# First layer: x and its norm placed ahead of the state tables, scale and shift by halves of the channels, the first products of w_in in two halves

## The chip, the cores and the metric

The kernel runs on one core of a Trainium2 chip. The time is the device time of one execution in microseconds (us), and of several executions the median is given. The core has TensorE (PE; its weight loads are listed as PEld), VectorE (DVE), ScalarE (ACT), GpSimd (POOL) and SyncE (SP), which here only issues DMA transfers. ACT issues DMA transfers too, on a queue of its own.

## The reference

A network of two layers on 256 tokens of 1024 channels, all in fp32. Each layer normalizes x, scales and shifts it by values that come from a conditioning vector c, runs a mixer (an S5 state-space layer in layer 0, an attention layer in layer 1), and then a PEER mixture of experts in the same manner:

```python
def rmsnorm(x, g):
    y = x * lax.rsqrt(jnp.mean(x * x, axis=-1, keepdims=True) + RMS_EPS)
    return y * g
...
    c_act = jax.nn.silu(c)
    for i in range(DEPTH):
        mod = c_act @ ada_w[i] + ada_b[i]
        sh1, sc1, g1, sh2, sc2, g2 = jnp.split(mod, 6, axis=-1)
        hm = rmsnorm(x, norm1_g[i]) * (1.0 + sc1) + sh1
        y = s5_mixer(hm, ...) if i % 2 == 0 else nsa_mixer(hm, ...)
        x = x + g1 * y
        hf = rmsnorm(x, norm2_g[i]) * (1.0 + sc2) + sh2
        x = x + g2 * peer(hf, ...)
    return rmsnorm(x, final_g)
...
def s5_mixer(h, w_in, a_re, a_im, log_dt, b_re, b_im, c_re, c_im, d_skip, w_glu):
    u = h @ w_in
    # powers of exp(a * dt), times b and c, give a recurrence over the tokens for each of 64 groups
```

## The kernel before

x is held transposed in one tile `xT`: 128 partitions by 8 chunks (k) of 128 channels by 256 tokens. Products with the big weights are made of three fp32r products (`mm3`, L188 to L190): a weight block of 128x1024 arrives in a buffer `raw` (`load_unit`, L129, a 512 KB transfer on SP's queue into one of six buffers), ACT rounds it to `w_hi` in two halves of four chunks (L139), DVE subtracts to get `w_lo` (L181), and PE adds w_hi x h_hi, w_hi x h_lo and w_lo x h_hi.

What the start of layer 0 has to make, and the lines that the profile shows for it:

- `Tables(K, pp)` clears the tiles of the state tables. `s5_params` (L359 to L420) turns the parameters in `prm` into coefficients: on ACT an exp (L383), a tanh (L387) and two sines (L395, L396), on DVE a long run of 128x32 operations.
- `sq_all`: eight squares of xT on ACT (L249) and their sums over the channels on PE (L260, products with ones).
- `ada_block(K, 0, n)`: 512 of the 6144 values of mod. Four loads of ada_w, eight products with the column `cact` = silu(c) (L201), a row copied by ACT (L204); the call of what it returns (`ada_turn`) turns the row by products with ones (L213), and DVE adds the bias into `mod` (L216). Blocks 0 and 1 are the shift for chunks 0 to 3 and 4 to 7, blocks 2 and 3 the scale. silu is made of a sigmoid on ACT (L118) and a DVE product (L119).
- `rms_scale`: mean on DVE (L273), square root on ACT (L274), reciprocal and a diagonal on DVE (L275, L277), and a PE product with ones (L279) that spreads the result over the partitions: `rs`, in PSUM.
- `Norm`: `nsc` = (1 + scale) * g on DVE (L290); `scaled(k)` makes `nt` = xT * nsc * rs on DVE (L297); `shifted(k)` adds the shift, `h_hi` on ACT (L303) and `h_lo` on DVE (L304).
- `tab.first(0)`: angles, sines and cosines of the first quarter of the groups (L464 to L475), `bpad` by complex products on DVE and POOL (L450 to L455), its 16 PE transposes (L489) and four ACT copies to `win` (L490). `tab.second(0)`: `wo` (L501, L455) and T (L512 on PE, L516 on ACT).
- `Pair`: loads and splits of the first two blocks of w_in; `add(k)` makes the six products of chunk k.

`tc.manual_schedule(engines={PE, Activation})` in `s5_layer` keeps the instructions of the block on PE and ACT in the order in which they are written. DVE, POOL, SP and everything outside the block is ordered by the compiler's planner, which goes by simulated time and priority; `high_priority(offset=...)` raises what stands in it. Within a queue, every engine works in order. `s5_mix` then goes through the eight blocks of w_in with the states of each, and the tables of later quarters; the planner places some of their DVE and ACT work before that.

Of the kernel before, what the change touches and what calls it, by code (L numbers as in the profile page):

```python
# [14 lines left out]
OP = mybir.AluOpType  # L15
# [5 lines left out]
KC = D // P  # L21
DEPTH = 2
EPS = 1e-6
PRIO = 200
# [85 lines left out]
def small(K, name):  # L110
    o, w = SMALLS[name]
    return K.sm[:, o:o + w]
# [9 lines left out]
def bank(K):  # L122
    return K.ps.tile([P, 512], F32, name="bank")


def load_unit(K, src):

    t = K.st.tile([P, 1024], F32, name="raw", bufs=RAW)
    K.nc.sync.dma_start(t, src)  # L129
    return t  # L130
# [13 lines left out]
def split_w(K, raw):  # L144

    with K.tc.high_priority(offset=PRIO):
        return [split(K, raw[:, i * 512:(i + 1) * 512], [P, 512], "w", bufs=4) for i in range(2)]
# [10 lines left out]
class Pair:  # L158


    def __init__(self, K, srcs, x):
        self.K, self.x = K, x
        self.ws = [split_w(K, load_unit(K, src)) for src in srcs]
        self.ps = [bank(K)[:, :S] for _ in srcs]
# [28 lines left out]
def ada_block(K, layer, n):  # L193

    nc = K.nc
    ps = bank(K)
    for k2 in range(KC // 2):
        w = load_unit(K, K.aps["ada_w"][n, k2]).rearrange("p (k n) -> p k n", k=2)
        for i in range(2):
            k = 2 * k2 + i  # L200
            nc.tensor.matmul(ps[32 * (k % 4):32 * (k % 4) + 32], K.cact[:, k, :], w[:, i, :],  # L201
                             start=(k < 4), stop=(k >= 4), skip_group_check=True)
    row = K.xp.tile([P, 512], F32, name="ada_row", bufs=1)
    nc.scalar.activation(row, ps, AF.Copy)  # L204
    return lambda: ada_turn(K, layer, n, row)
# [58 lines left out]
def sq_all(K):  # L264
    for k in range(KC):
        sq_add(K, k)


def rms_scale(K):

    nc = K.nc
    ms = K.xp.tile([P, 2], F32, name="ms")
    nc.vector.tensor_scalar(ms, K.sq[:, 0:2], 1.0 / D, EPS, op0=OP.mult, op1=OP.add)  # L273
    nc.scalar.activation(ms, ms, AF.Sqrt)  # L274
    nc.vector.reciprocal(ms, ms)  # L275
    diag = K.xp.tile([P, 2, P], F32, name="rs")
    nc.vector.tensor_mul(diag, K.ident[:, None].to_broadcast([P, 2, P]), ms[:, :, None].to_broadcast([P, 2, P]))  # L277
    rs = bank(K)[:, :S]
    nc.tensor.matmul(rs, K.ones, diag.rearrange("p t n -> p (t n)"), start=True, stop=True)  # L279
    return rs  # L280


class Norm:


    def __init__(self, K, g, layer, part, rs, bufs=4):
        self.K, self.part, self.rs, self.bufs = K, part, rs, bufs
        self.mod = K.mod[layer]
        self.sc = K.xp.tile([P, KC], F32, name="nsc")
        K.nc.vector.scalar_tensor_tensor(self.sc, self.mod[:, part + 8:part + 16], 1.0, g, op0=OP.add, op1=OP.mult)  # L290
        self.hi = K.hpool.tile([P, KC, S], F32R, name="h_hi")
        self.lo = K.hpool.tile([P, KC, S], F32R, name="h_lo")
        self.t = K.xp.tile([P, KC, S], F32, name="nt")

    def scaled(self, k):
        K = self.K
        K.nc.vector.scalar_tensor_tensor(self.t[:, k % self.bufs], K.xT[:, k], self.sc[:, k:k + 1], self.rs,  # L297
                                         op0=OP.mult, op1=OP.mult)
# [29 lines left out]
NP2 = 32  # L328
# [7 lines left out]
S5_W = 3 * NP2 + 4 * NP2 * 16  # L336
# [185 lines left out]
def s5_layer(K):  # L522
    tc, nc = K.tc, K.nc
    with tc.tile_pool(name="s5p", bufs=1, reuse_waits="tile") as pp:
        prm = pp.tile([P, S5_W], F32, name="prm")
        nc.sync.dma_start(prm, K.aps["s5p"])
        nc.sync.dma_start(K.xT, K.aps["xT"])
        tab = Tables(K, pp)
        with tc.manual_schedule(engines={mybir.EngineType.PE, mybir.EngineType.Activation}):
            s5_params(K, pp, prm)  # L530
            sq_all(K)
            ada_block(K, 0, 2)()
            ada_block(K, 0, 3)()
            rs = rms_scale(K)
            tab.first(0)
            norm = Norm(K, small(K, "n1g")[:, 0:8], 0, 0, rs, KC)
            with tc.high_priority(offset=2 * PRIO):
                for k in range(KC):
                    norm.scaled(k)
            h = (norm.hi, norm.lo)  # L540
            ada_block(K, 0, 0)()
            pair = Pair(K, [K.aps["w_in"][0], K.aps["w_in"][1]], h)
            ada_block(K, 0, 1)()
            with tc.high_priority(offset=2 * PRIO):
                for k in range(4):
                    norm.shifted(k)
            with tc.high_priority(offset=2 * PRIO):
                for k in range(4, KC):
                    norm.shifted(k)
            for k in range(4):  # L550
                pair.add(k)
            for k in range(4, KC):
                pair.add(k)
            tab.second(0)
        s5_mix(K, pp, h, tab, pair.ps)

# [860 lines left out]
```

## Time and profile before

| | us |
|---|---|
| median of 3 runs | 2096.19 |
| lowest, highest | 2095.28, 2097.87 |
| the profiled execution, its own time | 2095.41 |
| its span from the first to the last instruction | 2093.6 |
| PE busy | 2036.0 (97%) |
| DVE busy | 1611.3 (77%) |
| ACT busy | 1154.3 (55%) |

The profile is one execution, recorded by the hardware. Times in it count from the start of the span. A busy share is an average over the whole span; the first 57 us, which the change touches, look different from the rest. "Idle before" is the time in which the engine had nothing running ahead of a row's first instruction, with the engine and line that ended it. Landings of a transfer are given from its issue. DMA from a queue runs on 16 DMA engines.

### The profile page before, as it was taken

What the parts mean: (1) busy time and instruction counts of PE and PEld (TensorE: products, weight loads), DVE (VectorE), ACT (ScalarE), POOL (GpSimd) and SP (SyncE); (2) the same over time, 40 slices, a digit from 0 to 9 for tenths busy, and PEclk for the clock granted to TensorE, in tenths of its full rate; (3) what the DMA queues carried; (4) which work ended last, traced back from release to release, by engine and by line L of the source; (5) the groups of instructions that cost most, each with busy time, mean ns of one, the idle gap of its engine ahead of it and who ended that gap; (6) DMA issues with size and microseconds to landing.
All of it is one profiled execution on the core that took longest, in us unless ns stands there. A gap on an engine that the chain in (4) does not pass through costs nothing. (4 is left out here: it accounts for less than half of the span.)

```text
span 2093.6 us, 39285 instructions
## 1 busy us (share of the span) xinstructions
PE 2036.0 (97%) x14344; PEld 1842.8 (88%) x14344; DVE 1611.3 (77%) x3698; ACT 1154.3 (55%) x2396; POOL 113.3 (5%) x149
## 2 busy tenths in 40 slices
PE   6899999999999999999999999999999999999998
PEld 3789999899999988888888689999999998888887
DVE  8696899878887777777766769998788865566555
ACT  4775555554445555555545655555454455555554
POOL 4220001200000000000010000022000000000000
PEclk9899999999999999999999999999999999999999
DMA  7445555544446788888863035555444455666663
GB/s 282 149 180 162 162 173 172 160 151 135 140 140 190 260 271 274 267 269 272 270 221 101 21 129 165 172 171 162 141 132 142 141 177 184 194 193 196 193 192 100
DMA packets 102690, 377.18 MB, mean 180 GB/s; under 512 B 11488, under 2 KB 11872, under 8 KB 101472
## 3 DMA queue, kind: packets, MB, share of 16 engines
q1 hardware_dynamic: 101520, 371.42, 55.8%
q0 software_dynamic: 544, 2.61, 0.4%
q8 instruction: 112, 1.84, 0.3%
q14 instruction: 82, 0.67, 0.1%
q10 hardware_dynamic: 432, 0.65, 0.1%
HBM read 373.07 MB, written 1.05 MB: 179 GB/s over the span
## 5 line engine op out<-in xcount | busy, mean ns | idle before, releaser
L139 ACT ACTIVATE w_hi<-raw 128x512 fp32r<-128x512 f32 x1194 | 746.8, 628 | 737.8 <-PE bank L189 433.5
L181 DVE TENSOR_TENSOR w_lo<-raw,w_hi 128x512 fp32r<-128x512 f32 x1194 | 814.9, 704 | 132.5 <-ACT w_hi L139 130.2
L188 PE MATMUL bank<-h_hi,w_hi 128*128 128x256 f32 x2504 | 717.3, 289 | 9.0 <-ACT w_hi L139 5.6
L190 PE MATMUL bank<-h_hi,w_lo 128*128 128x256 f32 x2504 | 709.1, 286 | 10.7 <-DVE w_lo L181 10.7
L189 PE MATMUL bank<-h_lo,w_hi 128*128 128x256 f32 x2504 | 709.5, 284 | 1.4 <-DVE h_lo L304 1.4
L188 PEld LDWEIGHTS bank<-h_hi,w_hi 128*128 128x128 f32 x2504 | 485.2, 195 | 17.1 <-ACT w_hi L139 7.5
L190 PEld LDWEIGHTS bank<-h_hi,w_lo 128*128 128x128 f32 x2504 | 480.2, 193 | 15.3 <-DVE w_lo L181 14.7
L189 PEld LDWEIGHTS bank<-h_lo,w_hi 128*128 128x128 f32 x2504 | 483.1, 193 | 3.8 <-DVE h_lo L304 2.7
L799 PE MATMUL bank<-w_lo,a_hi 128*128 128x512 f32 x1024 | 399.0, 390 | 0.2 <-DVE w_lo L181 0.2
L799 PE MATMUL bank<-w_hi,a_lo 128*128 128x512 f32 x1024 | 398.5, 389 | 0.0
L799 PE MATMUL bank<-w_hi,a_hi 128*128 128x512 f32 x1024 | 281.0, 390 | 0.0
L181 DVE TENSOR_TENSOR a_lo<-B,a_hi 128x256 fp32r<-128x256 f32 x256 | 108.9, 425 | 197.9 <-ACT a_hi L139 197.8
L799 PEld LDWEIGHTS bank<-w_hi,a_lo 128*128 128x128 f32 x1024 | 192.3, 188 | 39.8
L799 PEld LDWEIGHTS bank<-w_lo,a_hi 128*128 128x128 f32 x1024 | 192.3, 188 | 39.8 <-DVE w_lo L181 0.7
L799 PEld LDWEIGHTS bank<-w_hi,a_hi 128*128 128x128 f32 x1024 | 191.5, 188 | 38.6
L770 PE MATMUL bank<-ohl,oij 128*128 128x128 f16 x1024 | 129.2, 307 | 0.0
L139 ACT ACTIVATE a_hi<-B 128x256 fp32r<-128x256 f32 x256 | 106.7, 418 | 27.0 <-PE bank L799 14.4
L773 DVE SCALAR_TENSOR_TENSOR B<-bank,B 128x216 f32<-128x216 f32 (+31 forms) x128 | 62.5, 488 | 71.9 <-PE bank L770 71.1
L770 PEld LDWEIGHTS <-oij 128*128 128x128 f16 x1024 | 101.5, 128 | 4.2
L762 DVE TENSOR_TENSOR oij<-iota,slotT 128x1024 f16<-128x1024 f16 x128 | 89.2, 698 | 0.0
L765 DVE TENSOR_TENSOR ohl<-oij,slotT 128x1024 f16<-128x1024 f16 x128 | 88.8, 695 | 0.1
L233 DVE SCALAR_TENSOR_TENSOR raw<-raw,cb 128x1024 f32<-128x1024 f32 x56 | 68.3, 1219 | 0.0
(263 smaller groups left out, 1790.2 us busy)
## 6 DMA issues: line engine op xcount, KB each, us to landing
raw<-peer_u SPq DMA_DIRECT2D x256, 512.0 KB, 3.6
raw<-peer_v SPq DMA_DIRECT2D x256, 512.0 KB, 4.3
raw<-ada_t SPq DMA_DIRECT2D x56, 512.0 KB, 4.6
raw<-ada_w SPq DMA_DIRECT2D x40, 512.0 KB, 5.4
raw<-w_q SPq DMA_DIRECT2D x32, 512.0 KB, 3.5
raw<-w_glu SPq DMA_DIRECT2D x16, 512.0 KB, 4.1
raw<-w_in SPq DMA_DIRECT2D x8, 512.0 KB, 6.3
w<-w_cmp SPq DMA_DIRECT2D x4, 1024.0 KB, 9.4
```

Source lines behind the costliest of these rows:

```text
L139: nc.scalar.activation(hi, raw, AF.Copy)
L181: K.nc.vector.tensor_tensor(lo, raw, hi.bitcast(F32), op=OP.subtract)
L188: nc.tensor.matmul(out, wh, xh, start=start, stop=False)
L189: nc.tensor.matmul(out, wh, xl, start=False, stop=False)
L190: nc.tensor.matmul(out, wl, xh, start=False, stop=stop)
L233: V.scalar_tensor_tensor(w, w, 1.0, cb, op0=OP.mult, op1=OP.mult, accum_out=part[:, m:m + 1])
L762: V.tensor_tensor(oij.rearrange("p a n j t -> p (a n) j t"), tab[:, None].to_broadcast(full), si, op=OP.is_equal)
L765: V.tensor_tensor(ohl, oj, slotT[:, 1, 2 * q:2 * q + 2, :, None, :].to_broadcast([P, 2, 2, P, 2]), op=OP.mult)
L770: nc.tensor.matmul(pv[:, :, t], oij[:, t // 2, 0, :, t % 2], ohl[:, t // 2, n, :, t % 2], start=(n == 0), stop=(n == 1), skip_group_check= ...
L773: V.scalar_tensor_tensor(B[:, :jd, ts], pv[:, :jd], 1.0 / GS, B[:, :jd, ts], op0=OP.mult, op1=OP.mult)
L799: nc.tensor.matmul(acc[t][dh], a[al][:, ts], w[wl], start=(j == 0 and al + wl == 0), stop=(j == NJ - 1 and al == 1))
```

## The change

In the new code xT is loaded first on SP's queue. The parameters `prm` move to ACT's queue, behind sm and cst, and in two transfers: the first 96 columns (a_re, a_im, log_dt) and the other 2048 (b and c). Inside the ordered block, after `s5_params`, come the squares and the norm (`rms_scale`), with raised priority. Then, in two rounds of four chunks each: the scale block of ada (2, then 3) and the half of `nsc` and four `scaled`; the shift block (0, then 1) and four `shifted`; the products of these four chunks. All of it has raised priority. The loads and splits of w_in stand behind the first four `shifted`. `tab.first(0)` comes between the two rounds, `tab.second(0)` after the second. `Norm` gets an argument `late` and a method `scales` for half of `nsc`. The instructions are the same but for one transfer and one small DVE operation more.

```diff
--- before.py
+++ after.py
@@ -283,14 +283,20 @@
 class Norm:
 
 
-    def __init__(self, K, g, layer, part, rs, bufs=4):
+    def __init__(self, K, g, layer, part, rs, bufs=4, late=False):
         self.K, self.part, self.rs, self.bufs = K, part, rs, bufs
-        self.mod = K.mod[layer]
+        self.mod, self.g = K.mod[layer], g
         self.sc = K.xp.tile([P, KC], F32, name="nsc")
-        K.nc.vector.scalar_tensor_tensor(self.sc, self.mod[:, part + 8:part + 16], 1.0, g, op0=OP.add, op1=OP.mult)
+        if not late:
+            self.scales(0, KC)
         self.hi = K.hpool.tile([P, KC, S], F32R, name="h_hi")
         self.lo = K.hpool.tile([P, KC, S], F32R, name="h_lo")
         self.t = K.xp.tile([P, KC, S], F32, name="nt")
+
+    def scales(self, k0, k1):
+        p = self.part + 8
+        self.K.nc.vector.scalar_tensor_tensor(self.sc[:, k0:k1], self.mod[:, p + k0:p + k1], 1.0, self.g[:, k0:k1],
+                                              op0=OP.add, op1=OP.mult)
 
     def scaled(self, k):
         K = self.K
@@ -523,34 +529,37 @@
     tc, nc = K.tc, K.nc
     with tc.tile_pool(name="s5p", bufs=1, reuse_waits="tile") as pp:
         prm = pp.tile([P, S5_W], F32, name="prm")
-        nc.sync.dma_start(prm, K.aps["s5p"])
         nc.sync.dma_start(K.xT, K.aps["xT"])
+        for cs in (slice(0, 3 * NP2), slice(3 * NP2, S5_W)):
+            nc.scalar.dma_start(prm[:, cs], K.aps["s5p"][:, cs])
         tab = Tables(K, pp)
+        first = lambda: K.tc.high_priority(offset=2 * PRIO)
         with tc.manual_schedule(engines={mybir.EngineType.PE, mybir.EngineType.Activation}):
             s5_params(K, pp, prm)
-            sq_all(K)
-            ada_block(K, 0, 2)()
-            ada_block(K, 0, 3)()
-            rs = rms_scale(K)
-            tab.first(0)
-            norm = Norm(K, small(K, "n1g")[:, 0:8], 0, 0, rs, KC)
-            with tc.high_priority(offset=2 * PRIO):
-                for k in range(KC):
-                    norm.scaled(k)
+            with first():
+                sq_all(K)
+                rs = rms_scale(K)
+            norm = Norm(K, small(K, "n1g")[:, 0:8], 0, 0, rs, KC, late=True)
             h = (norm.hi, norm.lo)
-            ada_block(K, 0, 0)()
-            pair = Pair(K, [K.aps["w_in"][0], K.aps["w_in"][1]], h)
-            ada_block(K, 0, 1)()
-            with tc.high_priority(offset=2 * PRIO):
-                for k in range(4):
-                    norm.shifted(k)
-            with tc.high_priority(offset=2 * PRIO):
-                for k in range(4, KC):
-                    norm.shifted(k)
-            for k in range(4):
-                pair.add(k)
-            for k in range(4, KC):
-                pair.add(k)
+            pair = None
+            for half in range(2):
+                with first():
+                    for n in (2 + half, half):
+                        ada_block(K, 0, n)()
+                        ks = range(4 * half, 4 * half + 4)
+                        if n > 1:
+                            norm.scales(ks[0], ks[-1] + 1)
+                            for k in ks:
+                                norm.scaled(k)
+                        else:
+                            for k in ks:
+                                norm.shifted(k)
+                    if not half:
+                        pair = Pair(K, [K.aps["w_in"][0], K.aps["w_in"][1]], h)
+                    for k in ks:
+                        pair.add(k)
+                if not half:
+                    tab.first(0)
             tab.second(0)
         s5_mix(K, pp, h, tab, pair.ps)
```

## Rows read from the trace of the kernel before

**Rows 1.** Table of stretches: length, busy us of each engine, granted clock, DMA share.

```profile
17.64:28.94 11.30, 9.74 (x49) 3.95 (x48) 10.77 (x43) 2.28 (x3) 6.22 (x13) 1.00 0.72 240
...
48.12:56.82 8.70, 8.01 (x54) 7.47 (x57) 7.72 (x18) 3.34 (x10) 4.10 (x8) 0.80 0.55 224
```

**Rows 2.** Timeline of PE: start, us, line, operation, count, idle before.

```profile
10.72 6.99 PE L260 MATMUL bank<-ones,sq 128*128 128x1 f32 x32 [10.72 <-DVE iota L62]
17.64 3.64 PE L201 MATMUL bank<-raw,cact 128*32 128x512 f32 x16
...
32.34 1.22 PE L279 MATMUL bank<-rs,ones 128*128 128x256 f32 x2 [3.40 <-DVE rs L277]
33.35 3.60 PE L489 MATMUL bank<-cst,bpad 128*128 128x128 f32 x16
36.89 1.92 PE L201 MATMUL bank<-raw,cact 128*32 128x512 f32 x16
...
47.20 1.05 PE L213 MATMUL bank<-ones,ada_row 128*128 128x1 f32 x8 [0.76 <-ACT ada_row L204]
```

**Rows 3.** Timeline of ACT, the same columns.

```profile
6.10 0.23 ACT L383 ACTIVATE sp<-prm 128x32 f32<-128x32 f32 x1 [3.15 <-DMA prm<-s5p]
6.35 1.28 ACT L118 ACT_TABLE_LOAD   x1
...
10.02 0.23 ACT L395 ACTIVATE sp<-sp 128x32 f32<-128x32 f32 x1
...
10.27 1.01 ACT L249 ACTIVATE sq<-xT 128x256 f32<-128x256 f32 x3
...
27.24 0.60 ACT L204 ACTIVATE ada_row<-bank 128x512 f32<-128x512 f32 x1 [5.28 <-PE bank L201]
...
29.15 0.20 ACT L274 ACTIVATE ms<-ms 128x2 f32<-128x2 f32 x1
...
39.40 2.18 ACT L139 ACTIVATE w_hi<-raw 128x512 fp32r<-128x512 f32 x4
...
47.05 1.69 ACT L303 ACTIVATE h_hi<-nt,mod 128x256 fp32r<-128x256 f32 x4
```

**Rows 4.** Timeline of DVE, the same columns.

```profile
19.24 0.15 DVE L273 TENSOR_SCALAR ms<-bank 128x2 f32<-128x2 f32 x1
...
31.66 0.16 DVE L275 RECIPROCAL ms<-ms 128x2 f32<-128x2 f32 x1
...
41.45 0.69 DVE L181 TENSOR_TENSOR w_lo<-raw,w_hi 128x512 fp32r<-128x512 f32 x1
...
47.81 0.62 DVE L304 SCALAR_TENSOR_TENSOR h_lo<-nt,mod,h_hi 128x256 fp32r<-128x256 f32 x1
...
51.44 0.15 DVE L216 TENSOR_TENSOR mod<-bank,sm 128x4 f32<-128x4 f32 x1
```

**Rows 5.** DMA issues of the first 12 us: count, KB, us to landing.

```profile
prm<-s5p SPq DMA_DIRECT2D x1, 1072.0 KB, 5.3
xT<-xT SPq DMA_DIRECT2D x1, 1024.0 KB, 7.8
cst<-consts ACTq DMA_DIRECT2D x1, 128.0 KB, 8.0
sm<-smalls ACTq DMA_DIRECT2D x1, 76.0 KB, 5.5
```

**Rows 6.** DMA queues (q1 SP's, q10 ACT's), 3 to 4 us: packets, MB.

```profile
q1 hardware_dynamic: 42, 0.36, 85.7%
q10 hardware_dynamic: 43, 0.03, 10.2%
```

**Rows 7.** Table of stretches during the products with w_in, two granted clocks.

```profile
50.60:53.60 3.00, 3.00 (x16) 3.00 (x16) 2.92 (x9) 1.98 (x5) 1.28 (x3) 0.50 0.76 307
54.00:56.40 2.40, 2.40 (x22) 2.40 (x21) 2.25 (x6) 0.07 (x1) 1.02 (x2) 1.00 0.01 3
```

**Rows 8.** DMA issues of the whole span: count, KB, median us to landing.

```profile
raw<-ada_w SPq DMA_DIRECT2D x40, 512.0 KB, 5.4
```

## Prediction

> **What bounds the kernel now.** I read the table of stretches for the first 57 us, then the timelines of PE, ACT and DVE for the same time, then the DMA landings. The change touches only what happens before the last product with the first two blocks of w_in, which ends at 56.82 us of a span of 2093.6. After that point nothing in the code is changed, so what counts is how far that end moves; I pass it on one to one, since the work behind it starts from these products.
>
> Up to that end PE follows one written order. The sums of squares run from 10.72 (32 instructions in 6.99 us), ada blocks 2 and 3 from 17.64, and the norm's product L279 stands at 32.34 behind an idle 3.40 us that DVE's rs ended; then come 16 transposes, ada block 0 at 36.89, block 1, and the 48 products [rows 1, 2]. Why so late? The mean square was read at 19.24 by DVE, yet ScalarE took its square root only at 29.15: its queue holds instructions in written order, and the row copy of block 3, at 27.24, had waited 5.28 us for PE [rows 3, 4]. DVE then took the reciprocal at 31.66, 2.3 us after the root's end. So block 0, whose weights were asked for long before, waits for the norm. DVE is busy 10.77 of 11.30 us in the stretch of the first two ada blocks: whatever needs it stands in line [rows 1].
>
> **The change, step by step.** Three things move: the load order, the norm's place, and the split of scale, shift and products into halves.
>
> *Loads.* Now prm is first on SP and lands at 0.75+5.3 = 6.05; xT second, at 1.19+7.8 = 9.0; sm and cst on ACT's queue land at 6.25 and 9.2 [rows 5]. Afterwards xT is first on SP and takes prm's place, about 6.2. The parameters that s5_params needs first (96 columns, 48 KB) become third on ACT's queue. The packets of the two queues alternate one by one: 42 against 43 in one microsecond, 8.5 KB against some 0.6 KB [rows 6]. So cst landed with xT although it has an eighth of the bytes, as 256 packets of SP's had to pass. The new third transfer waits for 384 packets of SP's (xT, two ada loads): 2.1 MB, as before cst. I put it at 9.3 (bounds 9.0 and 10), 3.2 us later than prm now. The Trainium skill (DMA: Bandwidth & Descriptors, Specifications) says that transfers under 512 B lose line rate, and these rows have 384 B; no row here shows such a packet, and twice the time for 8 packets an engine would add an estimated 0.3 us.
>
> *Parameters ahead of squares.* In the new text s5_params still stands ahead of sq_all, so ScalarE still does exp, tanh and two sines before the first square. Exp goes from 6.10 to 9.3. From exp to the first square there are 4.17 us now, of which the table load at 6.35 and the sigmoid that it serves take some 1.5 [rows 3]. Sm lands first, so I put the sigmoid ahead of exp and count 2.7 (upper bound 4.2): first square at 12.0, against 10.27. That xT is there at 6.2 then buys nothing. PE's sums take 0.45+6.92: end at 19.4, against 17.64.
>
> *The norm's chain* now stands between sums and ada block 2. Its parts: mean 0.15, root 0.20, 0.68 from the reciprocal's start (31.66) to the product's (32.34), 1.0 from there to its successor at 33.35, and some 0.3 for hand-overs: 2.3 us [rows 2, 3, 4]. The root's table load hides behind the last sums. The lateness of DVE comes on top: 1.5 us before the mean (19.24, sums done at 17.7), 2.3 before the reciprocal; together an upper bound of 6.1. With raised priority the nearest row is w_lo, which is raised already: it came at 41.45, 1.5 after its w_hi was there, while the first h_lo, raised too, came at 47.81, 0.3 after its h_hi. I take 0.8 for each lateness: 3.9, and block 2 starts on PE at 23.3, against 17.64. The 3.40 us idle of L279 goes, and this wait takes its place.
>
> *Blocks 2 and 0 with their turns*: 11.30 us, as blocks 2 and 3 have now [rows 1]; their loads fit in the six buffers or come before use. End at 34.6.
>
> *First half.* The shift needs mod: 0.15 and 0.8 late, 35.6. Four h_hi take 1.69 (37.3), and w_hi now stands behind them; the third, which the second block's product needs, ends at 38.9 (2.18 for four) [rows 3]. On DVE four h_lo of 0.62, from 36.0, and three w_lo of 0.69 [rows 4] end about 40.6. Now w_hi and w_lo were ready while block 1 was awaited; here they are on the path. 18 products are left: 2.0 us at 0.11 each at a granted clock of 1.00, 3.4 at 0.19 and 0.50 [rows 7]. At the higher level, 42.6.
>
> *Transposes and block 3.* The 16 transposes took 3.60 us at the low clock [rows 2]; half that at 2.4 GHz: 44.4. Block 3 takes 1.92 as at 36.89, its row copy and hand-overs 0.8, its turn 1.05: 48.2.
>
> *Block 1.* Its last two loads need buffers that block 3 gives back at 44.9 and 45.3; at the median of 5.4 us to landing [rows 8] they come at 50.3 and 50.7, and products, row copy and turn end at 53.0 (without the wait for the loads 52.0).
>
> *Second half.* Mod 0.95, first h_hi 0.5, then 24 products: the 48 took 8.70 us now, 0.18 each with both clocks [rows 1], so 4.3 (2.6 to 4.6): end at 58.8. The scales and the four scaled of each half hide behind block 0 and block 1 on PE; without that cover they would cost 1.6 a half. Memsets, moved table work and the larger part of prm cost nothing on this path: DVE has table work for later quarters ahead of need.
>
> **Sum.** 58.8 against 56.82: 2.0 us later. The start of block 2 loses 5.7; the stall of 3.40, the wait of block 0 behind the first transposes, and products of the first half ahead of block 1 give most of it back. The profiled execution took 2095.41, 0.8 below the median of 2096.19 and inside the runs' spread. So 2098.2 against the median. 0.2% is 4.2 us, about what a measurement of this kernel can tell from no change.
>
> With no lateness on DVE (1.6 at the norm, 0.7 at each mod), 2.6 for the last products and loads in time, the sum is 5.7 less: 2092.5; with all upper bounds at once it is beyond 2108.
>
> **Rivals.**
> *ScalarE is not held by the parameters.* If squares start when xT lands, at 6.4 in place of 12.0, all moves 5.6 us ahead: end at 53.2. With DVE free of backlog at the norm (1.6) it is 51.6: 5.2 less than now, 2091.0. Against it: the root at 29.15 kept its written place though its input was 10 us old. It decides with a first square before 7.4 or so. Chance 0.16.
>
> *DVE's lateness stays as the rows show it*, in every hand-over of the new chain: 1.5 and 2.3 at the norm, 1.5 at the first mod (as w_lo), 3.2 at the second (mod at 51.44, its turn done at 48.25 [rows 2, 4]). That is 5.3 more than I counted: 2103.5. For it: DVE is busy 95% there. Against it: the mods were not raised then. It makes the kernel slower from a mean lateness of 1.4 us on. Chance 0.20.
>
> *The clock.* Both bursts of products and the transposes run at 1.2 GHz, as the 3 us from 50.60 did behind the thin stretch of block 1, since each burst now follows a wait of some 3 us: 1.4 for the first half, 1.8 for the transposes, 1.7 for block 3 (3.64 against 1.92 [rows 2]), 0.3 for the second: 5.2 more, 2103.4. Chance 0.09.
>
> *The split of prm is no split*: s5_params waits for both transfers. The large one, 128 packets of 8 KB between as many of an ada load, 1.6 MB at the 0.39 MB of that microsecond [rows 6], lands some 4.1 us later: 2102.3. Chance 0.05.
>
> **How the numbers follow.** The forecast case has 0.50, with 2093 to 2100 as its own range, within 0.2%. Faster has the first rival, 0.16; slower the other three, 0.34. The range 2091 to 2104 leaves out about half of the first rival and the upper tails of the second and third, 0.18.
>
> **What would show it.** In the changed profile: the small part of prm lands near 9.3 and exp starts there; the first square near 12, well after xT landed; L279 about 4 us behind the end of the sums; block 2 on PE near 23; first products near 38; last products near 58 to 59. A first square before 8, or a last product before 54, would make the forecast wrong on the fast side; mod or reciprocal more than 1.5 us behind their inputs, or last products after 61, on the slow side. A difference that arises after that end would show that the delay is not passed on one to one.

## The result: slower by 0.75%, and x is loaded seventh

| | before | changed |
|---|---|---|
| median (lowest to highest) of 4 runs, same chip | 2096.85 us (2095.28 to 2097.87) | 2112.44 us (2111.03 to 2113.76) |
| span of the profiled execution | 2093.6 | 2111.0 |
| last product with the first two blocks of w_in ends | 56.82 | 72.21 |

The ratio is 1.0075, interval 1.0063 to 1.0087: some 15.6 us slower, where 2098.2 with a range to 2104 was forecast. The last product is 15.4 us late, and the eight gate activations behind the mixer, which began at 165.5 to 200.1 before, begin 15.0 late: the loss lies in the first layer's head, before that product. Executions of one kernel differ by up to 10 us, and some traced ones are the slowest of their kernel, so the traces are read up to that product, and medians with their intervals.

What SP issues in the changed kernel (timeline of SP's queue), and when its loads landed (DMA issues of the first 14 us; the last column is us from issue to landing):

```profile
0.75 4.94 SPq L129 DMA_DIRECT2D raw<-ada_w  x6
6.16 0.33 SPq L532 DMA_DIRECT2D xT<-xT  x1
```

```profile
raw<-ada_w SPq DMA_DIRECT2D x6, 512.0 KB, 7.0
prm<-s5p ACTq DMA_DIRECT2D x1, 1024.0 KB, 10.3
xT<-xT SPq DMA_DIRECT2D x1, 1024.0 KB, 10.4
...
prm<-s5p ACTq DMA_DIRECT2D x1, 48.0 KB, 7.0
```

Six ada loads go out first, and x is the seventh: it was issued at 6.16 and landed at 16.5; before, it landed at 9.0 [rows 5]. In the text x's load stands first. But `first()` raises the priority of all that is written inside it, and `ada_block` issues its own loads there; x's load is written outside. The planner that fills SP's queue takes the raised ones first. So the change does not do what it says, and "loaded first" in the section on the change holds for the text alone.

ACT (timeline), to set beside [rows 3]:

```profile
8.69 0.23 ACT L389 ACTIVATE sp<-prm 128x32 f32<-128x32 f32 x1 [2.37 <-DMA prm<-s5p]
...
16.55 1.03 ACT L249 ACTIVATE sq<-xT 128x256 f32<-128x256 f32 x3 [1.02 <-DMA xT<-xT]
...
31.11 0.20 ACT L274 ACTIVATE ms<-ms 128x2 f32<-128x2 f32 x1 [7.85 <-DVE ms L273]
```

DVE and PE (timelines), to set beside [rows 4] and [rows 2]:

```profile
28.42 2.05 DVE L461 TENSOR_TENSOR wo<-cm,cm 64x256 f32<-64x256 f32 x4
...
30.93 0.15 DVE L273 TENSOR_SCALAR ms<-bank 128x2 f32<-128x2 f32 x1
...
32.55 0.17 DVE L275 RECIPROCAL ms<-ms 128x2 f32<-128x2 f32 x1
...
40.07 0.16 DVE L216 TENSOR_TENSOR mod<-bank,sm 128x4 f32<-128x4 f32 x1 [6.49 <-PE bank L213]
```

```profile
17.02 6.99 PE L260 MATMUL bank<-ones,sq 128*128 128x1 f32 x32 [17.02 <-ACT sq L249]
33.63 1.22 PE L279 MATMUL bank<-rs,ones 128*128 128x256 f32 x2 [9.63 <-DVE rs L277]
34.79 3.44 PE L201 MATMUL bank<-raw,cact 128*32 128x512 f32 x16
...
52.48 1.91 PE L495 MATMUL bank<-cst,bpad 128*128 128x128 f32 x16
54.32 1.92 PE L201 MATMUL bank<-raw,cact 128*32 128x512 f32 x16
57.94 1.50 PE L213 MATMUL bank<-ones,ada_row 128*128 128x1 f32 x8 [1.70 <-ACT ada_row L204]
59.37 3.64 PE L201 MATMUL bank<-raw,cact 128*32 128x512 f32 x16
```

The exp that needed the 48 KB ran at 8.69, and ScalarE's first square came at 16.55, when x was there: 4.5 us later than forecast. The sums of squares ended at 24.01, yet DVE took the mean at 30.93: table work that the planner had placed ahead of it (L461 and the like) stood in front for 6.9 us. With x first that wait is 2.3 us (x_first, below), so the late x costs twice. TensorE idles 9.63 us ahead of L279, where it idled 3.40 before, and block 2 starts at 34.79, not 17.64. In the stretch 24 to 36 us the DMA engines moved nothing: the six buffers held weights of blocks that waited for the norm.

```profile
24.00:36.00 12.00, 2.37 (x11) 0.90 (x14) 9.03 (x22) 0.20 (x1) 6.97 (x13) 1.00 0.00 0
```

(Table of stretches; columns as in [rows 1]: PE 2.37, DVE 9.03 of 12 us busy; clock 1.00; DMA share 0.00.)

### The profile page after: what moved, and what is told of

The parts are those of the page before. It is cut to its first block, busy times and chain, and to the rows that moved or that the text cites. A ratio compares the mean times of both kernels' runs of the same rounds, so it can differ in the third digit from the quotient of the medians.

```text
span 2111.0 us, 39288 instructions
## 1 busy us (share of the span) xinstructions
PE 2036.4 (96%) x14344; PEld 1843.3 (87%) x14344; DVE 1612.1 (76%) x3699; ACT 1154.5 (55%) x2396; POOL 113.1 (5%) x149
## 3 DMA queue, kind: packets, MB, share of 16 engines
q8 instruction: 112, 1.84, 0.4%
HBM read 373.07 MB, written 1.05 MB: 177 GB/s over the span
## 5 line engine op out<-in xcount | busy, mean ns | idle before, releaser
L190 PEld LDWEIGHTS bank<-h_hi,w_lo 128*128 128x128 f32 x2504 | 481.0, 193 | 16.1 <-DVE w_lo L181 15.6
```

Source lines behind the costliest of these rows:

```text
L190: nc.tensor.matmul(out, wl, xh, start=False, stop=stop)
```

## Experiments

All kernels in one table, ratios with their intervals against runs of the kernel before on the same chip; "last" is the end of the last product with the first two w_in blocks in the one traced execution, "L279" the start of the norm's product there, "DVE" its busy time until "last", from the table of stretches.

| kernel | median us | ratio | L279 | last | DVE |
|---|---|---|---|---|---|
| before | 2096.85 | 1 | 32.34 | 56.82 | 50.98 |
| changed | 2112.44 | 1.0075 [1.0063, 1.0087] | 33.63 | 72.21 | 50.37 |
| x_first | 2103.62 | 1.0035 [1.0021, 1.0049] | 25.78 | 65.19 | 50.01 |
| loads_only | 2096.81 | 1.0005 [0.9996, 1.0015] | 34.31 | 57.21 | 49.62 |
| norm_ahead_no_halves | 2101.47 | 1.0025 [1.0015, 1.0035] | 25.36 | 62.82 | 51.59 |
| squares_first | 2106.71 | 1.0042 [1.0025, 1.0059] | 18.27 | 64.81 | 49.46 |
| tables_behind_norm | 2100.5 | 1.0023 [1.0011, 1.0034] | 20.70 | 62.00 | 49.38 |
| norm_beside_blocks | 2095.97 | 1.0002 [0.9992, 1.0012] | 30.05 | 56.78 | 50.77 |
| after_tables_behind_norm | 2107.9 | 1.0058 [1.0041, 1.0075] | 25.24 | 66.23 | 49.61 |
| turn_before_tables | 2106.76 | 1.0052 [1.0035, 1.0068] | 20.54 | 65.54 | 48.90 |
| before_fewer_adds | 2096.04 | 0.9997 [0.9987, 1.0006] | 29.69 | 55.16 | 43.12 |
| beside_fewer_adds | 2095.56 | 0.9993 [0.9982, 1.0003] | 30.12 | 54.91 | 43.21 |
| behind_fewer_adds | 2100.25 | 1.0018 [1.0008, 1.0027] | 20.67 | 59.15 | 44.24 |
| beside_adds_gpsimd | 2098.64 | 1.0011 [1.0001, 1.002] | 27.78 | 58.97 | 49.77 |
| whole_products_tables_behind | 2097.77 | 1.0003 [0.9994, 1.0013] | 20.64 | 58.06 | 50.87 |
| turn0_before_tables | 2095.88 | 0.9998 [0.9989, 1.0007] | 29.02 | 54.04 | 47.88 |
| tables_behind_scaled | 2106.65 | 1.0036 [1.0024, 1.0049] | 20.37 | 62.27 | 49.08 |

### Which part of the change loses

**x_first**: the changed kernel, with x's load above the raised ada loads.

```
-        nc.sync.dma_start(K.xT, K.aps["xT"])
+        with tc.high_priority(offset=4 * PRIO):
+            nc.sync.dma_start(K.xT, K.aps["xT"])
```

> The changed kernel with one edit: the load of xT is raised above the six raised loads of ada_w, so that it stands first on SP's queue. Theory (load order): in the changed kernel xT was issued seventh, at 6.16 us, and landed at 16.5; the squares waited for it, and the planner, which knew it to be late, put the mean behind the table work of DVE. With xT first it lands at about 6.2, the first square runs at 11 to 12 behind the sines, the mean is read within 2 us of the sums' end, L279 stands at 21 to 24 in place of 33.6, and the last product with the first two blocks of w_in ends at 59 to 62 in place of 72. Time 2098 to 2102. Rival (long chain): norm, scale, shift and products one behind the other are long in themselves, whatever the load order; then the time stays above 2106. Rival (DVE's backlog): the mean stays some 7 us behind the sums, time 2103 to 2106.

2103.62: 8.8 us of the 15.6 are gone in the medians, and 7.0 at the last product. x landed 5.6 after an issue at 0.75. The theory had the place right and missed its numbers, 59 to 62 for the last product (65.19) and 2098 to 2102; the time lies in the range of the rival on DVE's backlog, which had the mean some 7 us late, where it was 2.3. The start now runs as the prediction said (first square at 12.01, sums to 19.45), and its own faults become visible (DVE, ACT and PE, timelines):

```profile
21.74 0.14 DVE L273 TENSOR_SCALAR ms<-bank 128x2 f32<-128x2 f32 x1
...
24.05 0.15 DVE L275 RECIPROCAL ms<-ms 128x2 f32<-128x2 f32 x1
24.12 0.16 DVE L375 TENSOR_TENSOR s5keep<-sp,sp 128x32 f32<-128x32 f32 x1
24.21 0.18 DVE L370 TENSOR_TENSOR s5keep<-sp,sp 128x32 f32<-128x32 f32 x1
24.31 0.95 DVE L461 TENSOR_TENSOR bpad<-cm,cm 64x256 f32<-64x256 f32 x2
25.30 0.42 DVE L277 TENSOR_TENSOR rs<-cst,ms 128x256 f32<-128x256 f32 x1
```

```profile
12.01 1.02 ACT L249 ACTIVATE sq<-xT 128x256 f32<-128x256 f32 x3
...
49.29 1.06 ACT L496 ACTIVATE win<-bank 128x512 f32<-128x512 f32 x2
50.24 0.60 ACT L204 ACTIVATE ada_row<-bank 128x512 f32<-128x512 f32 x1
```

```profile
25.78 1.22 PE L279 MATMUL bank<-rs,ones 128*128 128x256 f32 x2 [6.32 <-DVE rs L277]
...
50.89 1.84 PE L213 MATMUL bank<-ones,ada_row 128*128 128x1 f32 x8 [2.13 <-ACT ada_row L204]
52.66 3.64 PE L201 MATMUL bank<-raw,cact 128*32 128x512 f32 x16
```

Mean, reciprocal and diagonal each stand behind table work on DVE; raised priority did not put them in front. Block 3's row copy stands behind sines and window copies on ACT. Block 1's products take 3.64, at a granted clock of 0.50, and block 3's 1.92 at 1.00.

**loads_only**: the kernel before with x first on SP and prm in two on ACT's queue. **norm_ahead_no_halves**: the same with the norm ahead of blocks 2 and 3.

```
 loads_only:
-        nc.sync.dma_start(prm, K.aps["s5p"])
         nc.sync.dma_start(K.xT, K.aps["xT"])
+        for cs in (slice(0, 3 * NP2), slice(3 * NP2, S5_W)):
+            nc.scalar.dma_start(prm[:, cs], K.aps["s5p"][:, cs])
 norm_ahead_no_halves, besides:
             sq_all(K)
+            rs = rms_scale(K)
             ada_block(K, 0, 2)()
             ada_block(K, 0, 3)()
-            rs = rms_scale(K)
```

> The kernel before with the load order alone that the change wants: xT first on SP, prm in two parts on ACT's queue. Written order as before. Theory (load order): xT lands at 6.2 and the small part of prm at 8.7, exp and sines are 2.6 us later than before but lose the sigmoid between them, first square at 11 to 11.5 against 10.27; all of it small: 2095 to 2099, no difference from the kernel before. Rival (late parameters): DVE starts its parameter work 2.6 us later and everything shifts by it, 2099 to 2101.

> loads_only with one more edit: the norm's scale (rms_scale) is written ahead of ada blocks 2 and 3, as in the change, but scale, shift and products are not split into halves. It shares the loads with x_first and loads_only. Theory: blocks 2 and 3 start 3 to 5 us later on PE, but L279's stall of 3.4 behind them is gone and the transposes follow at once: 2095 to 2100. If the halves are what costs, x_first is 3 us or more above this run; if the norm's place is what costs, this run and x_first are both 3 us or more above loads_only.

The loads alone cost nothing (1.0005, the interval holds 1). The norm ahead costs 4.7 us in the medians and 5.6 at the last product; 2095 to 2100 was forecast. The halves, as x_first minus this, cost 2.2 more, which the interval of x_first does not tell from nothing (at the last product 2.4). In norm_ahead_no_halves nothing of the norm's chain is raised, and mean (21.35, sums done at 19.05) and reciprocal (23.63, root done at 21.72) were 2.3 and 1.9 us late; raised, in x_first, they were as late, 2.3 and 1.9.

**squares_first**: x_first with the squares ahead of the parameters on ScalarE, the condition of the first rival.

```
-            s5_params(K, pp, prm)
             with first():
                 sq_all(K)
+            s5_params(K, pp, prm)
+            with first():
                 rs = rms_scale(K)
```

> x_first with one more edit: the squares are written ahead of the state parameters, and the mean and root behind them, so that ScalarE does not hold the squares behind exp, tanh and sines. Theory: first square at 6.4 to 7, sums done at 14, L279 at 16 to 18, ada block 2 at 17 to 19, last products with the first two blocks at 53 to 56, time 2092 to 2097, 4 to 6 below x_first. Rival (DVE holds it): the mean stands ahead of the parameters on DVE and the parameters behind the squares on ScalarE, so tables come later; then the gain is lost at the transposes and the time is within 2 us of x_first.

The rival was right: the first square came at 6.39 and L279 at 18.27, 7.5 us ahead of x_first, and at the last product 0.4 us are left of it. The trace (ACT, then DVE, timelines) shows where they went: with the parameters later, more of the table work is still to do, and the low parts of w_in stand among it. The medians of four and five runs, 2106.71 and 2103.62, do not tell the two apart.

```profile
6.39 1.03 ACT L249 ACTIVATE sq<-xT 128x256 f32<-128x256 f32 x3 [1.94 <-DMA xT<-xT]
```

```profile
36.52 0.68 DVE L181 TENSOR_TENSOR w_lo<-raw,w_hi 128x512 fp32r<-128x512 f32 x1
37.12 0.41 DVE L456 TENSOR_TENSOR cm<-s5keep,prm 128x256 f32<-128x256 f32 x1
37.46 0.68 DVE L181 TENSOR_TENSOR w_lo<-raw,w_hi 128x512 fp32r<-128x512 f32 x1
38.06 0.84 DVE L461 TENSOR_TENSOR wo<-cm,cm 64x256 f32<-64x256 f32 x2
38.94 1.50 DVE L181 TENSOR_TENSOR w_lo<-raw,w_hi 128x512 fp32r<-128x512 f32 x2
```

### Is it DVE's queue?

**tables_behind_norm** is x_first, **after_tables_behind_norm** the changed kernel, with DVE's table work queued behind the norm's diagonal (an order of issue, no wait).

```
-    nc.vector.tensor_mul(diag, ...
+    K.last_rs = nc.vector.tensor_mul(diag, ...
...
                 if not half:
-                    tab.first(0)
-            tab.second(0)
+                    with tc.issue_after(K.last_rs.ins):
+                        tab.first(0)
+            with tc.issue_after(K.last_rs.ins):
+                tab.second(0)
```

> x_first with one thing more: on VectorE every instruction of the state tables is queued behind the norm's diagonal, so that mean, reciprocal and diagonal no longer stand behind them. In x_first the sums of squares ended at 19.45, the mean began at 21.74, the root at 21.92, the reciprocal at 24.05, the broadcast product at 25.78. Theory (VectorE's queue is what the norm's chain waits for): the mean comes within 0.3 us of the sums' end, the reciprocal within 0.3 us of the root, the broadcast product at 21 to 21.7, block 2 at 22.5; if nothing behind gives it back, the last product of w_in comes at 61 instead of 65.1 and the median at 2099.5 (2098.5 to 2101). Rival (the table work is only moved, and VectorE has no room): the broadcast product comes early all the same, but the new mod of block 2, the low parts of w_in or the transposes come later by what was moved, and the last product stays at 64 to 66, the median at 2102.5 to 2104.5.

> The changed kernel as it is (x loaded seventh on its queue) with the state tables queued behind the norm's diagonal on VectorE. There the sums of squares ended at 24.01 and the mean began at 30.93, the broadcast product at 33.63. Theory (the later x came, the more table work stood ahead of the mean, so that the late x cost twice): the mean at 24.1, the broadcast product at 25.6 to 26.2, 7.5 us earlier; of these 5 to 8 us reach the last product (72.1 before), the median at 2104.5 to 2107.5. Rival (the table work moved behind the norm delays mod and the low parts of w_in by as much): the last product at 70 to 73, the median at 2110.5 to 2113.

The norm's chain closes up in both (DVE of after_tables_behind_norm, then DVE and PE of tables_behind_norm, timelines):

```profile
24.14 0.16 DVE L273 TENSOR_SCALAR ms<-bank 128x2 f32<-128x2 f32 x1 [5.78 <-PE bank L260]
24.57 0.17 DVE L275 RECIPROCAL ms<-ms 128x2 f32<-128x2 f32 x1 [0.27 <-ACT ms L274]
```

```profile
30.75 0.16 DVE L216 TENSOR_TENSOR mod<-bank,sm 128x4 f32<-128x4 f32 x1
```

```profile
20.70 1.22 PE L279 MATMUL bank<-rs,ones 128*128 128x256 f32 x2 [1.20 <-DVE rs L277]
...
38.14 0.58 PE L188 MATMUL bank<-h_hi,w_hi 128*128 128x256 f32 x1 [6.56 <-ACT w_hi L139]
```

With x late this is worth 8.4 us at L279, 6.0 at the last product and 4.5 in the median (2107.9, just above the forecast); with x first 5.1, 3.2 and 3.1. The rest is handed back: TensorE now idles 6.56 us ahead of the first product of w_in, since mod and scale wait behind the tables (block 2's turn ended at 26.47, its mod came at 30.75). In tables_behind_norm the norm's chain takes 2.3 us from the sums' end (19.51) to block 2 (21.85), the 2.3 that the prediction summed for its parts.

**turn_before_tables**: tables_behind_norm with the first tables written behind block 3's turn, their priority not raised.

```
                             for k in ks:
                                 norm.scaled(k)
+                            if half:
+                                tables()    # tab.first(0), as above
...
-                if not half:
-                    with tc.issue_after(K.last_rs.ins):
-                        tab.first(0)
```

> tables_behind_norm with one thing more: the first group's tables are written behind block 3 and its turn instead of ahead of block 3, so that block 3's row copy on ScalarE no longer stands behind sines and copies of the tables. In x_first this row copy came at 50.24, and TensorE stood idle 2.13 us for it. Theory: the row copy follows block 3's products within 0.5 us, TensorE's wait ahead of that turn falls to about 0.8, and 1 to 2 us are gained on tables_behind_norm, at the last product and in the median (about 2098 where tables_behind_norm gives 2099.5). Rival (the tables are only later, and the mixer waits for them): the last product is as early, the mixer's first products of the states later by as much, and the median equals that of tables_behind_norm within 0.7 us.

Theory and rival both missed (PE, timeline):

```profile
55.12 1.36 PE L213 MATMUL bank<-ones,ada_row 128*128 128x1 f32 x8 [2.84 <-ACT ada_row L204]
```

Block 3's copy is no longer held (idle 0.81), but block 1's is, and its mod comes at 58.30 instead of 55.93. It is 3.5 us slower at the last product and 6 in the medians. The wait went one block on.

**norm_beside_blocks**: the kernel before, with mean, root and diagonal written ahead of blocks 2 and 3 and only L279 behind them.

```
             sq_all(K)
+            diag = rms_scale(K)
             ada_block(K, 0, 2)()
             ada_block(K, 0, 3)()
-            rs = rms_scale(K)
+            rs = rms_bcast(K, diag)
```

> The kernel before with one thing alone: mean, root, reciprocal and diagonal are written ahead of blocks 2 and 3, while the broadcast product on TensorE stays behind block 3, so the blocks run while the norm is made. Theory (the 3.40 us that TensorE stood idle ahead of the broadcast product came from ScalarE's root behind both row copies, and a norm made beside the blocks costs TensorE nothing): the root at about 19.6, the broadcast product straight behind block 3's turn at about 29 instead of 32.34, all that follows up to 3.4 us earlier, the median at 2093.5 (2092.5 to 2095). Rival (VectorE's table work sets the time of the transposes and of the low parts of w_in, so that what the norm gives is handed back there): the broadcast product comes early, the last product of w_in within 1 us of 56.82 as before, the median 2095.5 to 2097.5.

The rival was right. The stall of 3.40 at L279 is gone, and nothing is gained, as two waits open behind it (PE, timeline; L284 is L279 here):

```profile
30.05 1.20 PE L284 MATMUL bank<-rs,ones 128*128 128x256 f32 x2
...
38.58 1.05 PE L213 MATMUL bank<-ones,ada_row 128*128 128x1 f32 x8 [2.69 <-ACT ada_row L204]
...
48.70 0.58 PE L189 MATMUL bank<-h_lo,w_hi 128*128 128x256 f32 x1 [2.60 <-DVE h_lo L309]
```

In all ten kernels so far DVE had been busy 48.9 to 51.6 us by the last product, wherever that lay. That looked like a law: the end is DVE's work plus its idle time. Four kernels tested it. **before_fewer_adds**, **beside_fewer_adds** and **behind_fewer_adds** leave out one of two additions of each product of the first two of the four groups of tables, in the kernel before, norm_beside_blocks and tables_behind_norm; **beside_adds_gpsimd** moves eight of them to GpSimd.

```
+            if g and hs.start < 2 * QP:
+                continue
             nc.vector.tensor_add(out[r, :, :, g, :], m0[r], m1[r])
 beside_adds_gpsimd, instead:
+            eng = nc.gpsimd if g and share else nc.vector    # share: second(0), second(1)
+            eng.tensor_add(out[r, :, :, g, :], m0[r], m1[r])
```

> The kernel before, with one of the two VectorE additions of each state-table product left out in the first two of the four groups of tables (part of the computation is left out; 15 additions of 0.46 us lie ahead of the last product of w_in, 6.9 us). In all ten kernels so far VectorE was busy for 48.8 to 51.6 us by the time of that last product, wherever it lay between 56.8 and 72.1. Theory (VectorE's queue sets the end of the stage, not TensorE's): the reciprocal and the broadcast product come about 2 us earlier and the low parts of h follow their mod, so that the last product comes 3 to 5 us earlier and the median falls to 2092 to 2094.5. Rival (TensorE's chain of blocks, row copies and turns sets it, and the additions fill time in which VectorE would wait): the last product within 1 us of 56.8, the median 2095.5 to 2097.5.

> norm_beside_blocks with the same additions left out as in before_fewer_adds (part of the computation is left out). With all the additions the early norm gained nothing: 2095.97 against 2097.02. Theory (VectorE's queue hid that gain): with the additions gone part of TensorE's 3.4 us comes through, and this is 0.7 to 2.5 us faster than before_fewer_adds. Rival: it equals before_fewer_adds within 0.7 us, so that the early norm is worth nothing for another reason.

> tables_behind_norm (x first, the changed order, tables queued behind the norm) with the same additions left out (part of the computation is left out). In tables_behind_norm the new mod of block 2 began 4.3 us after its turn, and TensorE stood idle 6.56 us ahead of the first product of w_in; six of the additions stood between the diagonal and that mod. Theory (VectorE's queue): the mod comes 2.8 us earlier, the first product at 35.3 instead of 38.14, the last at 59 instead of 61.9, the median at 2097.5 (2096 to 2099); it stays slower than before_fewer_adds by 2.5 to 5 us, since in this order VectorE also waits for the other engines in the second half. Rival (the changed order is slower only because VectorE has so much to do): it comes within 1.5 us of before_fewer_adds.

> norm_beside_blocks with one of the two additions of each product of the second set of tables (first two groups, 8 additions of 0.46 us on VectorE ahead of the last product of w_in) on GpSimd instead, nothing left out. On GpSimd a product of 128x128 took 0.58 us, so an addition of 64x256 is put at 1.1 us, an estimate by elements per partition; its queue has room, 25 of 57 us busy. Theory: VectorE is relieved of 3.7 us, and the last product comes 2 to 3 us earlier, the median at 2093.5 (2092 to 2095), faster than the kernel before. Rival (GpSimd becomes the wait: its additions delay its own products, on which VectorE waits): the last product within 0.7 us of 57 or later, the median 2095.5 to 2098.

The law fell. With 7.9 us less on DVE by then the kernel before gains 1.7 at the last product, between what theory and rival said, and nothing that can be measured in the median; the early norm on top adds 0.25. behind_fewer_adds gains 2.9 at the last product, as forecast (59.15), but its median, 2100.25, is that of tables_behind_norm. And on GpSimd the additions cost more than they relieve: 59.0, and 2098.6. So it is where an instruction stands in DVE's queue that counts; the amount of DVE's work bounds little.

### What is left

**whole_products_tables_behind**: norm_ahead_no_halves with the tables behind the norm, so tables_behind_norm without the halves. **tables_behind_scaled**: tables_behind_norm with the tables behind the first half's scaling instead.

```
 whole_products_tables_behind:
-            tab.first(0)
+            with tc.issue_after(K.last_rs.ins):
+                tab.first(0)
 tables_behind_scaled:
-        K.nc.vector.scalar_tensor_tensor(self.t[:, k % self.bufs], ...
+        K.last_rs = K.nc.vector.scalar_tensor_tensor(self.t[:, k % self.bufs], ...
```

> norm_ahead_no_halves (loads of x first, the norm ahead of blocks 2 and 3, the products of w_in taken whole) with the state tables queued behind the norm's diagonal on VectorE. norm_ahead_no_halves ran 2101.47 with the mean 1.9 us and the reciprocal 1.7 us late. Theory A (what is left of the loss, once x is first and the tables stand behind the norm, belongs to the halves): mean and reciprocal follow at once, the broadcast product comes at 21 instead of 25.4, and the kernel falls to 2096.5 to 2098, level with the kernel before and 2.5 to 4 us under tables_behind_norm (2100.5). Theory B (it belongs to the norm ahead of the blocks, which gives VectorE less time for the tables before the blocks' results come): it lies within 1.2 us of tables_behind_norm, 2099.3 to 2101.7.

> tables_behind_norm with the tables queued on VectorE behind the scaling of the first four channel tiles instead of behind the diagonal, so that mod and scale of block 2 do not wait behind table work (in tables_behind_norm the mod began 4.3 us after its turn, and TensorE stood idle 6.56 us ahead of the first product). Theory (VectorE's time is only moved: what the norm's chain and the first half gain, the tables lose, since VectorE now idles while the blocks run): the first product at 33 to 35 instead of 38.14, but the transposes ready no earlier than 44 to 47, the last product at 61 to 64, the median within 1.5 us of tables_behind_norm (2100.5). Rival (the chain to the first product is what the loss hangs on): the last product 3 us or more earlier than 61.9, the median at 2096.5 to 2098.

Theory A was right (its 1.9 and 1.7 for norm_ahead_no_halves are 2.3 and 1.9 in the trace): 1.0003 [0.9994, 1.0013], level with the kernel before, last product at 58.06 against 62.00. What is left of the loss belongs to the halves, with the order of blocks and the raised priority that come with them; these were not tried apart. In the written order of PE the first 24 products stand ahead of transposes, block 3 and block 1; while they wait the 6.56 us for DVE and ACT, all that could fill the time waits behind them. With the products whole, transposes and block 0 run in that time (PE, timeline):

```profile
30.58 1.05 PE L213 MATMUL bank<-ones,ada_row 128*128 128x1 f32 x8 [0.76 <-ACT ada_row L204]
31.50 1.95 PE L489 MATMUL bank<-cst,bpad 128*128 128x128 f32 x16
33.38 1.92 PE L201 MATMUL bank<-raw,cact 128*32 128x512 f32 x16
```

tables_behind_scaled brings the first product to 34.07, then its low parts are late (PE, timeline), and the last product stays at 62.27: moved, not gained.

```profile
34.07 0.58 PE L188 MATMUL bank<-h_hi,w_hi 128*128 128x256 f32 x1 [2.70 <-ACT w_hi L139]
...
37.96 0.58 PE L190 MATMUL bank<-h_hi,w_lo 128*128 128x256 f32 x1 [3.09 <-DVE w_lo L181]
```

So the 6.56 us wait alone is not what the halves cost: most of it went and the end stayed. That waiting products hold up the rest is argued from the traces, not shown by an edit of its own. Its runs lie between 2098.9 and 2108.7, with the traced one the fastest, so its median is not read.

**turn0_before_tables**: norm_beside_blocks with the tables behind block 0's turn.

```
             ada_block(K, 0, 0)()
+            tab.first(0)
             pair = Pair(K, ...
```

> norm_beside_blocks (the kernel before's loads and order; root, reciprocal and diagonal ahead of blocks 2 and 3) with the first group's tables written behind block 0 and its turn instead of ahead of block 0, so that block 0's row copy does not stand behind sines and window copies on ScalarE (TensorE stood idle 2.69 us ahead of that turn) and its products not behind the transposes. Theory (the early norm gained nothing because the wait moved to block 0's row copy): the turn of block 0 ends at about 36.5 instead of 39.6, the wait ahead of it falls to 0.8, and the last product of w_in comes 1 to 3 us earlier, the median at 2094 (2092.5 to 2095.5), faster than the kernel before. Rival (VectorE's additions of the tables between there and the low parts of h decide): the last product stays within 0.7 us of 56.7, the median 2095.5 to 2097.5.

The last product comes at 54.04, 2.8 us earlier, the best of all, and the wait ahead of block 0's turn is 0.76, as the theory said. The median, 2095.88, is 0.9998 [0.9989, 1.0007]: 16.6 us under the changed kernel, but above the theory's range and no proven gain on the kernel before. In its trace the lead over the kernel before was 3.1 us up to 1062 and 0.7 at 2084.

## Why the prediction was wrong

**Failed: "Loads".** "Afterwards xT is first on SP and takes prm's place, about 6.2": it was seventh and landed at 16.5. That the diff may not do what it says was a rival for prm's split alone, and not for x. The sums ended at 24.0, not 19.4, and DVE's table work then held the mean for 6.9 us. Share, by x_first: 7.0 us at the last product, 8.8 in the medians.

**Mis-sized: "The norm's chain".** 3.9 forecast, with bounds 2.3 and 6.1; 7.5 in x_first, 10.8 in the changed kernel (24.01 to 34.79). Its parts sum to the 2.3 of the lower bound when nothing stands ahead of them (tables_behind_norm). I took 0.8 for each lateness from raised rows; 2.3 and 1.9 came, and 1.1 at the diagonal, where I had none. The rival "DVE's lateness stays as the rows show it" had the place right at the norm; that its price, 2103.5, meets x_first's 2103.62 is luck, as the two mods that it priced were not late there (turns done at 37.02 and 58.97, mods at 37.06 and 59.01).

**Mis-sized: "Transposes and block 3", "Block 1".** From the end of the first products to the end of block 3's turn it took 7.7 in x_first, not 5.6: TensorE idled 2.1 for the row copy, which stood behind the tables on ACT (0.8 forecast), and the turn took 1.84, not 1.05, at a granted clock of 0.52. Block 1 took 6.3, not 4.8: the wait for its loads did not come, but its products took 3.64 at 0.50. The rival "The clock" had the effect, and its place in part: both bursts of products ran at means of 0.58 and 0.55, while the transposes and block 3's products, which it had slow too, ran at 1.00. A duration alone does not tell the level: block 2's products, too, took 3.64 in x_first, in a stretch for which the profile gives 1.00.

**Right, once x was first.** In x_first the exp started with its landed 48 KB at 9.71 (9.3), and the first square came at 12.01 (12.0), held by exp and sines as said; sums to 19.45 (19.4); "Blocks 2 and 0" 10.1 (11.3); prm's split a real split. That "First half" came at 8.0 (8.0) and "Second half" at 6.2 (5.8) is in part luck. In the first, the last low part of w_in was done 5.0 after block 0's turn, not 6.0, and the products ended 3.0 after that, not 2.0; in the second, the products began 0.8 after block 1's turn, not some 1.5, and took 5.4, not 4.3.

The sum there is 65.2, not 58.8: the 6.4 are 3.6 of the norm's chain, 2.1 of block 3 (1.3 ACT's row copy, 0.8 the turn), 1.5 of block 1 and 0.4 of the second half, less 1.2 of the blocks.

Of the Trainium skill's rule (DMA: Bandwidth & Descriptors, Specifications) that transfers under 512 B lose line rate no run here shows a row: the 48 KB landed 0.4 us later than forecast, near the 0.3 estimated by it, but the rest of the forecast landing was an estimate too.

Even with the load in the right place the change would have been slower, 1.0035.

**Rivals.** squares_first gave the faster rival its condition, a first square at 6.4, and it did not decide: end at 64.8, not 53.2. But the edit also put the parameters behind the squares, where the rival left them in place, so its price as stated was not tested.

**"I pass it on one to one"** held for the changed kernel (15.4 at the last product, 15.6 in the medians, with an interval of 13 to 18). For 2 to 3 us it is not shown either way. turn0_before_tables gains 2.8 at the last product, and its interval ends just short of that, at 2.3; behind_fewer_adds gains 2.9, and the intervals of the two kernels compared there are wider than that. From the last product to the end of the span the traced executions of all these kernels took 2034.8 to 2042.3 us, that of the kernel before 2036.8.

**Open:** whether gains of 2 to 3 us at the last product are lost behind it or only not resolved. In the traces the 15.4 us at the last product split into 7.0 for x's load, 3.2 for table work ahead of the norm once x is first, 3.9 for the halves once the tables are behind it, and 1.2 for the rest (whole_products_tables_behind against before). The medians give 8.8, 3.1, 2.7 and 0.9, each to some 2 or 3 us by the intervals, and the halves 2.2 when the tables stand in front.

## What to carry to other kernels

A raised priority raises everything traced under it, its loads too: after such an edit read the issue order of each DMA queue before anything else. A chain that crosses engines pays the queue of each engine at every hop; raising its first instruction does not clear the queue, while an order of issue behind its last one does. And work moved ahead on an in-order engine should be ready when its turn comes, since products that wait hold up everything written behind them (here read from traces, not tried alone).

## What was not expected of the hardware

A stretch of the same instructions, far behind the change, differed by 3 us between two executions, with the granted clock. Two tables of stretches, each up to the first copy of the keys (kt), of the kernel before and then of tables_behind_norm. The two were 7 us apart from 381 and 388 on up to 800 and 807:

```profile
800.00:1065.10 265.10, 261.94 (x1191) 217.80 (x1190) 201.81 (x389) 153.74 (x295) 3.91 (x9) 0.99 0.82 272
```

```profile
807.00:1075.20 268.20, 265.30 (x1195) 221.13 (x1193) 201.95 (x389) 153.67 (x295) 3.91 (x9) 0.97 0.80 269
```

The same number of instructions within the trace's gaps, a mean granted clock of 0.97 for 0.99, 3.1 us longer. In the trace of the changed kernel the same stretch took 265.0 us at 0.99, so a late end at 57 us does not by itself make it slow. A head start of 2 or 3 us at 57 us is no more than that.
